# A norm's first load issued before the attention results' loads, and attention's value products with a mixed base and stacked half-width corrections

## The chip, the core and the metric

The kernel runs on one core of a Trainium2 chip. The metric is the device time of one execution in microseconds (us), as a median over runs. One profiled execution of the kernel before is the source of all durations; engines are called as in the profile: PE (matrix products; PEld is its weight load), DVE (vector), ACT (scalar), POOL, and SP, which here only issues transfers.

## The reference

The program computes one step of a decoder layer for a prompt of 1024 tokens and 8 samples of 8 tokens each (together T = 1088 columns), in 32-bit floats, model width 1024:

```
xn = RMSNorm(x)
[q | k | v | glu_a | glu_b | gate_a | gate_b] = xn @ w_in
A  = window attention (window 128, 16 heads on 4 key-value heads, a learned sink per head) @ w_o_attn
B  = silu(LayerNorm(causal depthwise conv of 31 taps (glu_a * sigmoid(glu_b)))) @ w_pb
h  = x + (sigmoid(gate_a) * A + sigmoid(gate_b) * B) @ w_out
y  = h + convolutional feed-forward of RMSNorm(h); then a final RMSNorm
```

For a prompt query i of a block of 128, the window holds the keys j <= i of its own block and the keys j > i of the block before. So over a "ring" of 128 key places each place holds either the own or the previous block's key, and the output is sum over j of p[i, j] * (v_own[j] if j <= i, else v_prev[j]).

## The kernel before

**Number form.** A 32-bit operand is split in a high part (a rounded copy, type fp32r) and a low part (operand minus high part). `split_ps` (L244) does this with a copy on ACT (L245) and a subtraction on DVE (L246). A full product is three matmuls (`mm3`, L208: high-high L210, high-low L211, low-high L212).

**Order of the work.** A weight of 128 output rows is one "stream" (L214): for each of three chunks of 384, 384 and 320 columns it runs eight steps of three matmuls, and evacuates the bank. Each step calls `tick` (L562), which first issues all steps of the agenda that are due. So attention, the layer norm and weight splits are woven into the streams at tick counts written out by hand: per attention unit values at 8 (`A_VALUES`), scores at 0 and 5, transposition ("turn") at 14 and 20, the value products ("mix") at 21 and 27; units follow each other at distances of 19 to 22 ticks. A framework then schedules the whole program at build time: it fixes each engine's order, by the order in which the program issues instructions, shifted by `later(offset)` (L140; a negative offset is sooner), and by its own estimate of when they are ready, and it puts in all waits. The convolution is issued with `CONV_LATER` = 1200, so it fills what DVE has left.

**Weights.** `w_load` (L154) issues the load of a weight on SP (L159, tile `wraw`, two buffers), two weights ahead. For weights after the first five of the input projection `w_parts` (L167) makes the low part without DVE: ACT casts (L181) and negates (L182), and a transfer on POOL's queue adds the weight from memory to it (L183).

**Attention** (`attn_unit`, L424) is done for two pairs of key-value heads (p = 0, 1), eight blocks each, and two groups g of four heads in each unit. `values` (L434) splits the block's v into `vt[:, 0]` and, if there is a block before, the difference d = v_prev - v_own into `vt[:, 1]`. `scores` (L442) are products of 256 columns (L451, L452) followed by a softmax over the ring (ACT L418, L422). `turn` (L459) transposes p on PE (L463), splits it into a high and a low part (tile `pt`), and, with a block before, multiplies both by the mask j > i (one DVE instruction over 1024 elements, L471). `mix` (L476) runs two or four matmuls of 128 x 512 (L482): v with both parts of p, and d with both masked parts. Their output rows hold the high and the low half of v; an ACT copy (L487) and a DVE addition (L488) sum them. After g = 1 the result is split into q's own place (L491, L492) and its low part is completed by a transfer on POOL (L493). Units of samples (`sample_unit`, L510) are woven in the same way; their transposed p is copied by ACT (L536) to a tile of tag "av", which the units' results use too.

**After attention** (L1010 to L1028): when two gate weights are left, the agenda is drained, attention's pools are closed, and the results of p = 0, which were spilled to memory, are read back by six transfers on SP, three of `ah` (L1022) and three of `al` (L1023). With the last gate weight the layer norm of the convolution's outputs begins. Its four parts (`ln_steps`, L610) each have a `load` (two transfers `ct` <- `d_c`, L636), `first` (sums on DVE, L622), `center` (a mean over the channels as a product on PE, L630, that waits for the sums; subtraction L646; squares on ACT, L649; sums) and `apply` (the second mean on PE, L630 again; root and reciprocal L384 and L385; scaling L662; silu L664; splits). `LN_AT` (L88) has the ticks of the four steps, counted from the start of the last gate weight. After it come the streams of the attention output projection (`do_o`, L1066), which first load the stored gate rows `ga` (L1068) and take their sigmoid on ACT (L1069); their first operand is `ah`.

## Time and profile before

| | |
|---|---|
| median of three runs | 1641.32 us (1641.26 to 1644.25) |
| the profiled execution: its time | 1641.11 us |
| its span in the trace | 1639.3 us |
| PE busy | 1621.9 us (99%) |
| DVE, ACT, POOL busy | 1342.9 (82%), 911.9 (56%), 314.3 us (19%) |
| mean clock granted to PE | 0.997 |
| the value products (L482) | 120, first at 221, last at 592 us |
| the norm's loads (L636) | 8, from 610 to 692 us |

How to read the rows in the prediction: a row of the order in time has the start and the length in us, the engine, the line of the code, the operation, output <- input by tile names, the shape and a count; in brackets stands how long the engine was idle before, and what ended that. A row of waits has who waited <- for whom: total us, times, longest. A row of one line's instructions has the shortest, median and longest duration in ns. PE's durations overlap, since matmuls are pipelined: their cost is the distance from start to start. "SPq" is SP's queue of transfers.

### The profile page before, as it was taken

To read this page: it belongs to the slowest core of one execution; us is meant where nothing else is said; L and a number is where in the kernel's file an instruction comes from. 1 tells how busy PE (TensorE), PEld (TensorE's weight loads), DVE (VectorE), ACT (ScalarE), POOL (GpSimd) and SP (SyncE) were. 2 spreads that over 40 slices of the span, in tenths; PEclk is the share of its full clock that TensorE was granted. 3 is DMA by queue.
4 is the path that set the end of the run, shared out by engine and by line. 5 is a ranking of instruction groups with operands and counts; after the bars stand their busy time and mean duration, and the time that the engine had idled before them with its cause. 6 is when DMAs were issued, how large, how long until landed. Compare 5 with 4: busy or idle time off the path is not lost.

```text
span 1639.3 us, 30059 instructions
## 1 busy us (share of the span) xinstructions
PE 1621.9 (99%) x11428; PEld 1603.7 (98%) x11428; DVE 1342.9 (82%) x2395; ACT 911.9 (56%) x1964; POOL 314.3 (19%) x579
## 2 busy tenths in 40 slices
PE   9999999999999999999999999999999999999998
PEld 9999999999999998999999999999999999999997
DVE  7879669999999825788755999988888877989767
ACT  6536387885678854676532465555555555524332
POOL 0211122322133321111102432222222111000000
PEclk9999999999999999999999999999999999999999
DMA  6455455748645576548763632344444334766313
GB/s 211 106 130 122 102 117 91 169 84 193 143 92 127 130 187 219 175 157 229 185 228 105 212 119 68 110 120 118 119 117 115 100 110 152 247 162 158 108 62 110
DMA packets 124249, 229.90 MB, mean 140 GB/s; under 512 B 28360, under 2 KB 70344, under 8 KB 124088
## 3 DMA queue, kind: packets, MB, share of 16 engines
q1 hardware_dynamic: 88536, 140.12, 27.9%
q0 software_dynamic: 35136, 87.45, 23.2%
q8 instruction: 90, 1.47, 0.4%
q14 instruction: 55, 0.45, 0.1%
q10 hardware_dynamic: 432, 0.40, 0.1%
HBM read 157.47 MB, written 64.03 MB: 135 GB/s over the span
## 4 chain that ended last, share of the span: by engine, by line
PE 81%; DVE 5%; issue 5%; ACT 4%; DMA 3%; POOL 1%; SPq 0%; POOLq 0%; DVEq 0%; ACTq 0%
PE mm L212 19%; PE mm L210 19%; PE mm L211 19%; PE aux L210 6%; PE aux L212 6%; PE aux L211 6%; PE aux L482 1%; ACT ct L664 1%; DMA ct<-d_c 1%; ACT p L418 1%; PE aux L463 1%; PE aux L451 1%; PE aux L452 1%; DVE c L584 0%; DMA q<-av 0%
## 5 line engine op out<-in xcount | busy, mean ns | idle before, releaser
L210 PE MATMUL mm<-xh,whi 128*128 128x384 f32 (+1 forms) x904 | 300.7, 333 | 0.2 <-ACT xh L299 0.2
L212 PE MATMUL mm<-xh,wlo 128*128 128x384 f32 (+1 forms) x904 | 296.8, 328 | 0.9 <-DMA wlo<-wall 0.9
L211 PE MATMUL mm<-xl,whi 128*128 128x384 f32 (+1 forms) x904 | 297.1, 329 | 0.4 <-DVE xl L300 0.4
L211 PEld LDWEIGHTS mm<-xl,whi 128*128 128x128 f32 x904 | 170.9, 189 | 2.6 <-DVE xl L300 0.9
L210 PEld LDWEIGHTS mm<-xh,whi 128*128 128x128 f32 x904 | 170.9, 189 | 2.1 <-ACT xh L299 0.7
L212 PEld LDWEIGHTS mm<-xh,wlo 128*128 128x128 f32 x904 | 170.7, 189 | 2.1 <-DMA wlo<-wall 1.2
L1474 DVE SCALAR_TENSOR_TENSOR acc<-st,fc,acc 128x1104 f32<-128x1104 f32 x88 | 119.9, 1366 | 12.2 <-issue 6.7
L212 PE MATMUL mm<-th,wlo 128*128 128x272 f32 x320 | 92.3, 289 | 0.0
L211 PE MATMUL mm<-tl,wlo 128*128 128x272 f32 x320 | 92.3, 288 | 0.0
L210 PE MATMUL mm<-th,wlo 128*128 128x272 f32 x320 | 92.2, 288 | 0.0
L584 DVE SCALAR_TENSOR_TENSOR bt<-u,consts,bt 128x513 f32<-128x513 f32 x120 | 90.0, 750 | 0.5
L584 DVE SCALAR_TENSOR_TENSOR c<-sm,hsum,c 128x512 f32<-128x512 f32 x120 | 89.6, 746 | 0.1
L212 PE MATMUL mm<-mh,wlo 128*128 128x272 f32 (+4 forms) x304 | 88.9, 292 | 0.0
L584 DVE SCALAR_TENSOR_TENSOR c<-u,consts,c 128x512 f32<-128x512 f32 x112 | 83.6, 746 | 0.4 <-ACT c L595 0.3
L245 ACT CAST whi<-wraw 128x512 fp32r<-128x512 f32 x76 | 47.5, 625 | 62.8 <-DVE wraw L1670 29.9
L1819 ACT COPY st<-mm 128x272 f32<-128x272 f32 (+2 forms) x132 | 43.8, 349 | 55.9 <-PE mm L212 55.9
L245 ACT CAST wlo<-wraw 128x512 fp32r<-128x512 f32 x76 | 47.3, 624 | 41.0 <-PE mm L212 17.4
L1472 ACT ACTIVATE acc<-st,fc 128x1104 f32<-128x1104 f32 x44 | 57.6, 1315 | 15.3 <-DVE st L1775 11.8
L210 PE MATMUL aux<-mh,whi 128*128 128x272 f32 (+4 forms) x216 | 63.8, 295 | 0.0
L211 PE MATMUL aux<-ml,whi 128*128 128x272 f32 (+4 forms) x216 | 63.5, 294 | 0.0
L181 ACT CAST whi<-wraw 128x1024 fp32r<-128x1024 f32 x37 | 38.8, 1049 | 41.7 <-PE mm L211 40.6
L246 DVE TENSOR_TENSOR wlo<-wraw,wlo 128x512 fp32r<-128x512 f32 x76 | 52.8, 695 | 9.8 <-ACT wlo L245 9.1
(723 smaller groups left out, 5806.9 us busy)
## 6 DMA issues: line engine op xcount, KB each, us to landing
wraw<-wall SPq DMA_DIRECT2D x118, 512.0 KB, 3.9
wlo<-wall POOLq DMA_DIRECT2D x37, 512.0 KB, 6.6
bw<-d_b SPq DMA_DIRECT2D x42, 272.0 KB, 3.7
d_b<-gd POOLq DMA_DIRECT2D x36, 272.0 KB, 6.1
d_b<-acc POOLq DMA_DIRECT2D x24, 272.0 KB, 4.8
ar<-wdn SPq DMA_DIRECT2D x32, 192.0 KB, 3.9
d_g<-acc POOLq DMA_DIRECT2D x10, 544.0 KB, 4.8
ct<-d_c SPq DMA_DIRECT2D x8, 544.0 KB, 7.6
```

What stands on the lines that cost most here:

```text
L181: self.cast = self.nc.scalar.copy(h, r).ins
L210: mm(ps, wh, xh, start=first, stop=False, skip_group_check=more)
L211: mm(ps, wh, xl, start=False, stop=False, skip_group_check=more)
L212: self.last_mm = mm(ps, wl, xh, start=False, stop=last, skip_group_check=more).ins
L245: self.cast = self.nc.scalar.copy(h, src).ins
L246: self.low = self.nc.vector.tensor_tensor(l, src, h.bitcast(F32), ALU.subtract).ins
L418: nc.scalar.activation(pt[:, j, 0:WIN + 1], pt[:, j, 0:WIN + 1], AF.Exp, bias=nm[:, j:j + 1], accum_out=den[:, j:j + 1])
L451: nc.tensor.matmul(ps[:, j, :], q[g][:, h, qs], kd[g][:, keys], start=True, stop=False)
L584: mac = lambda o, x, w: nc.vector.scalar_tensor_tensor(o, x, w, o, ALU.mult, ALU.add)
L1472: nc.scalar.activation(acc, st[:, 0:AW], AF.Identity, bias=fb(f), scale=fw(f, 0))
L1474: nc.vector.scalar_tensor_tensor(acc, st[:, k:k + AW], fw(f, k), acc, ALU.mult, ALU.add)
L1819: self.evicted = (add if second and n == 0 and j == 1 else op)(d, r(banks[bank, j]))
```

## The change

Four things are changed.

1. **Value products.** The base of the ring is now mixed: rows 0 to 63 of `vt` are the own block's, rows 64 to 127 those of the block before. For queries of the first half (x = 0) only keys 0 to 63 can be wrong then, for the second half only keys 64 to 127. So a correction needs 64 keys for 64 queries of each of four heads; the high and the low part of the masked p are stacked on the 128 rows (`ptc`), against a tile `two` that holds the difference's 64 rows twice. `two` is filled by four transfers on SP from a tile `s` (tag "ts"). The mask `below` gets signs: the correction of the second half is own minus previous. p is transposed with its columns ordered by half, head, query, and the evacuation turns them back. A mix has two products of 512 columns and two of 256.
2. **The norm's first load** is issued right after the drain, ahead of the loads of `ah` and `al`; its `first` is due at tick 0 instead of 1 and its `center` at 15 instead of 17.
3. **Weight splits** of the kind L180 to L183 are issued with an offset of -100 (`WEIGHTS_SOONER`).
4. **The samples' transposed p** gets a tile of tag "ts" in place of "av".

```diff
@@ -72,6 +72,7 @@
 A_TURN = (14, 20)
 A_MIX = (21, 27)
 SPILL = 10
+WEIGHTS_SOONER = -100
 THIRD = 6
 S_STEPS = (0, 12, 18)
 NORM_LATER = (0, 0, 0, 42)
@@ -85,7 +86,7 @@
 W_PARTS = 4
 CONV_LATER = 1200
 TURN_SOONER = -60
-LN_AT = ((0, 1, 17, 36), (2, 37, 50, 80), (60, 81, 103, 134), (90, 135, 152, 183))
+LN_AT = ((0, 0, 15, 36), (2, 37, 50, 80), (60, 81, 103, 134), (90, 135, 152, 183))
 LEAD = (0, 0)
 FIRST_UNIT = (10, 16)
 SPACING = ({"u": 22, "s": 13}, {"u": 19, "s": 13})
@@ -178,9 +179,10 @@
         self.w_hl.append((h, l))
         if FIRST < i < self.n_in:
             def whole():
-                self.cast = self.nc.scalar.copy(h, r).ins
-                self.nc.scalar.activation(l, h.bitcast(F32), AF.Identity, scale=-1.0)
-                self.nc.gpsimd.dma_start(l, self.a["wall"][i], accum_op=ALU.add)
+                with self.later(WEIGHTS_SOONER):
+                    self.cast = self.nc.scalar.copy(h, r).ins
+                    self.nc.scalar.activation(l, h.bitcast(F32), AF.Identity, scale=-1.0)
+                    self.nc.gpsimd.dma_start(l, self.a["wall"][i], accum_op=ALU.add)
             return [whole]
 
         def part(x):
@@ -432,12 +434,18 @@
         vals = {}
 
         def values():
-            vt = vals["vt"] = self.t(self.at, [P, 2, 4, HD], "vt", F32R, bufs=2)
-            self.split_ps(vt[:, 0, 0:4:3, :], vt[:, 0, 1:3, :], self.v[:, blk, p])
+            vt = vals["vt"] = self.t(self.at, [P, 4, HD], "vt", F32R, bufs=2)
+            for r, y in ((slice(0, HD), blk), (slice(HD, P), blk - 1)) if blk else ((slice(0, P), 0),):
+                self.split_ps(vt[r, 0:4:3, :], vt[r, 1:3, :], self.v[r, y, p])
             if blk:
                 d = self.t(self.at, [P, 2, HD], "vd")
                 nc.vector.tensor_tensor(d, self.v[:, blk - 1, p], self.v[:, blk, p], ALU.subtract)
-                self.split_ps(vt[:, 1, 0:4:3, :], vt[:, 1, 1:3, :], d)
+                s = self.t(self.at, [P, 4, HD], "ts", F32R)
+                self.split_ps(s[:, 0:4:3, :], s[:, 1:3, :], d)
+                two = vals["two"] = self.t(self.at, [P, 2, 4, HD], "two", F32R, bufs=2)
+                for x in range(2):
+                    for y in range(2):
+                        nc.sync.dma_start(two[y * HD:y * HD + HD, x].bitcast(F32), s[x * HD:x * HD + HD].bitcast(F32))
 
         def scores(g):
             pt = live[g]["pt"] = self.t(self.at, [P, 4, WIN + 4], "p", bufs=2)
@@ -461,31 +469,39 @@
             ps = self.bank("aux")
             for h in range(4):
                 nc.tensor.transpose(ps[:, h * P:(h + 1) * P], pt[:, h, 0:P], self.ident)
-            x = self.t(self.at, [P, 2, 512], "pt", F32R)
-            parts = [(0, x[:, y]) for y in range(2)]
+            x = self.t(self.at, [P, 2, 2, 4, HD], "pt", F32R)
+            ph, pl = live[g]["parts"] = x[:, 0], x[:, 1]
             with self.later(TURN_SOONER if self.now - self.gated <= 3 else 0):
-                self.split_ps(x[:, 0], x[:, 1], ps)
+                self.split_ps(ph, pl, ps.rearrange("p (h x q) -> p x h q", h=4, x=2))
                 if blk:
-                    below = self.masks[:, None, WIN:2 * WIN].to_broadcast([P, 8, WIN])
-                    x0 = self.t(self.at, [P, 2, 512], "pt0", F32R)
-                    nc.vector.tensor_tensor(x0.rearrange("p y (a b) -> p (y a) b", a=4),
-                                            x.bitcast(F32).rearrange("p y (a b) -> p (y a) b", a=4), below, ALU.mult)
-                    parts += [(1, x0[:, y]) for y in range(2)]
-            live[g]["parts"] = parts
+                    c = live[g]["c"] = self.t(self.at, [P, 2, 4, HD], "ptc", F32R)
+                    side = self.masks[:, WIN:2 * WIN].rearrange("p (x q) -> p x q", x=2)
+                    pick = lambda o, x, m: nc.vector.tensor_tensor(o, x.bitcast(F32), m, ALU.mult)
+                    pick(c, ph, side[:, :, None, :].to_broadcast([P, 2, 4, HD]))
+                    for x in range(2):
+                        r, o = [slice(y * HD, (y + 1) * HD) for y in (x, 1 - x)]
+                        pick(c[o, x], pl[r, x], side[r, x, None, :].to_broadcast([HD, 4, HD]))
 
         def mix(g):
             r, o = [slice(x * HD, (x + 1) * HD) for x in (g, 1 - g)]
             av = self.bank("aux")
-            parts = live[g]["parts"]
-            for n, (y, x) in enumerate(parts):
-                v = vals["vt"][:, y, 2 * g:2 * g + 2, :].rearrange("p x d -> p (x d)")
-                nc.tensor.matmul(av, v, x, start=n == 0, stop=n == len(parts) - 1)
+            ph, pl = live[g]["parts"]
+            pair = lambda v: v[:, 2 * g:2 * g + 2, :].rearrange("p x d -> p (x d)")
+            flat = lambda x: x.rearrange("p a h q -> p (a h q)")
+            nc.tensor.matmul(av, pair(vals["vt"]), flat(ph), start=True, stop=False)
+            nc.tensor.matmul(av, pair(vals["vt"]), flat(pl), start=False, stop=True)
+            if blk:
+                for x in range(2):
+                    nc.tensor.matmul(av[:, x * 256:x * 256 + 256], pair(vals["two"][:, x]),
+                                     live[g]["c"][:, x].rearrange("p h q -> p (h q)"), start=False, stop=True,
+                                     skip_group_check=True)
             if g == 0:
                 live[0]["t"] = self.t(self.at, [P, 4 * P], "av", bufs=2).rearrange("p (a b) -> p a b", a=4)
             t = live[0]["t"]
-            av = av.rearrange("p (a b) -> p a b", a=4)
-            nc.scalar.copy(t[r], av[o])
-            nc.vector.tensor_tensor(t[r], av[r], t[r], ALU.add)
+            rows = lambda x: x.rearrange("p h (x q) -> p x h q", x=2)
+            cols = lambda x: x.rearrange("p (x h q) -> p x h q", x=2, h=4)
+            nc.scalar.copy(rows(t[r]), cols(av[o]))
+            nc.vector.tensor_tensor(rows(t[r]), cols(av[r]), rows(t[r]), ALU.add)
             if g == 1:
                 h, l = q[0][:, :, qs], q[1][:, :, qs]
                 nc.scalar.copy(h, t)
@@ -532,7 +548,7 @@
             tr = self.bank("aux")
             nc.tensor.transpose(tr[:, 0:P], pt[:, 0, 0:P], self.ident)
             nc.tensor.transpose(tr[:, P:2 * P], pt[:, 0, 64:192], self.ident)
-            ts = live["ts"] = self.t(self.at, [P, 4 * P], "av", bufs=2)[:, 0:2 * P]
+            ts = live["ts"] = self.t(self.at, [P, 2 * P], "ts")
             nc.scalar.copy(ts, tr[:, 0:2 * P])
 
         def mix():
@@ -655,7 +671,7 @@
             self.rstd(rstd, ps)
             self.ln_apply(i, n, live["ct"], rstd)
 
-        return [(self.now + at, f) for at, f in zip(LN_AT[i], (load, first, center, apply))]
+        return [(at, f) for at, f in zip(LN_AT[i], (load, first, center, apply))]
 
     def ln_apply(self, i, n, ct, rstd):
         nc = self.nc
@@ -1016,16 +1032,15 @@
                 a0_es = ExitStack()
                 a0 = pool(a0_es, "a0")
                 self.lt = pool(a0_es, "lt")
+                norms = [self.ln_steps(x) for x in range(KT // 2)]
+                norms[0].pop(0)[1]()
                 ah = self.t(a0, [P, 4, T], "ah", F32R)
                 al = self.t(a0, [P, 4, T], "al", F32R)
                 for (o, w) in CHUNKS:
                     nc.sync.dma_start(ah[:, :, o:o + w].bitcast(F32), self.d_ah[:, :, o:o + w].rearrange("j p t -> p j t"))
                     nc.sync.dma_start(al[:, :, o:o + w].bitcast(F32), self.d_al[:, :, o:o + w].rearrange("j p t -> p j t"))
             if n == self.n_in - 1:
-                steps = []
-                for x in range(KT // 2):
-                    steps += self.ln_steps(x)
-                self.plan(steps)
+                self.plan([(self.now + at, f) for steps in norms for at, f in steps])
             if kind == "b":
                 u = do_b(i)
             elif kind == "a":
@@ -2134,13 +2149,14 @@
 
     r = np.arange(P)
     ii, jj = r[:, None], np.arange(2 * WIN)[None]
-    above, below = [x.astype(np.float32) for x in (jj[:, :WIN] > ii, jj[:, :WIN] < ii)]
+    above = (jj[:, :WIN] > ii).astype(np.float32)
+    below = np.where(jj[:, :WIN] < HD, (jj[:, :WIN] < ii) & (ii < HD), -1.0 * ((jj[:, :WIN] >= ii) & (ii >= HD)))
     b, t = r // HD, r % NT
     past = np.arange(WIN)[None] > t[:, None]
     n = np.arange(NS)[None]
     new = [(n // NT == (2 * bp + b)[:, None]) & (n % NT <= t[:, None]) for bp in range(4)]
     ok = np.concatenate([past] + new, 1)
-    return np.concatenate([above, below, np.where(ok, 0.0, -1e30).astype(np.float32)], 1)
+    return np.concatenate([above, below.astype(np.float32), np.where(ok, 0.0, -1e30).astype(np.float32)], 1)
 
 
 def pack_consts(i):
```

## The prediction

> **What bounds the kernel now.** I read the page first, then who PE waited for, then the stretches, then order in time around each place where PE stood.
>
> ```profile
> PE 1621.9 (99%) x11428; PEld 1603.7 (98%) x11428; DVE 1342.9 (82%) x2395; ACT 911.9 (56%) x1964; POOL 314.3 (19%) x579
> ```
>
> ```profile
> PE aux L630 <- DVE sm L622: 3.8, 1, 3.8
> PE aux L451 <- ACT av L536: 1.7, 1, 1.7
> PE mm L212 <- DMA wlo<-wall: 0.9, 1, 0.9
> ...
> PE aux L482 <- DVE pt L246: 0.2, 1, 0.2
> ```
>
> ```profile
> 260.00:540.00 280.00, 276.39 (x1730) 268.15 (x1730) 270.67 (x486) 209.46 (x548) 70.96 (x102) 1.00 0.59 130
> 540.00:600.00 60.00, 60.00 (x380) 58.33 (x379) 37.16 (x75) 46.59 (x135) 18.90 (x28) 1.00 0.57 125
> 600.00:620.00 20.00, 20.00 (x125) 20.00 (x124) 0.00 (x0) 5.15 (x8) 3.67 (x6) 1.00 1.02 337
> ```
>
> PE has work nearly everywhere, so PE time that is taken out counts, and so do its few waits; the second view (total, times, longest) holds those that this change can touch. In the stretches the columns are length, then busy time of PE, PEld, DVE, ACT and POOL, granted clock, DMA share and GB/s. During attention DVE is nearly as full as PE (270.67 of 280), but it has 22.8 us free in 540 to 600 and is wholly free in 600 to 620, where the DMA engines are full (1.02, 337 GB/s). So attention is bound by PE with DVE close behind, and the stretch around 620 by transfers.
>
> **Part 1: the corrections on PE.** Each of 28 mixes (14 units with blk > 0, two groups) had four products of 512 columns; now it has two of 512 and two of 256. The matmul's own duration misleads, since matmuls overlap; what counts is the distance from start to start.
>
> ```profile
> 235.72 1.10 PE L482 MATMUL aux<-pt,vt 128*128 128x512 f32 x4
> 236.65 0.34 PE L210 MATMUL mm<-xh,whi 128*128 128x384 f32 x1
> ```
>
> ```profile
> 502.77 0.28 PE L451 MATMUL aux<-kd,q 128*128 128x256 f32 x1
> 503.01 0.28 PE L451 MATMUL aux<-kd,q 128*128 128x256 f32 x1
> ```
>
> ```profile
> L482 PEld LDWEIGHTS aux<-pt,vt x120: 186/188/247, 220.9 to 591.5; 128*128 128x128 f32 x120
> ```
>
> Four products took 236.65 - 235.72 = 0.93, 0.232 us each. One 256-column score product (L452) lies between the two L451 rows, so 0.12 each. 56 products times (0.232 - 0.12) is **6.2 us** off PE. Bounds: 0.12 is for the same shape with a weight load of its own, so more than this is hardly to be had; the other end is that the weight load of 188 ns sets the spacing, 56 x (0.232 - 0.188) = 2.5 us. I take 6.2, since the nearest row (L451) is of the very shape.
> The Trainium skill, "TensorE: Matmul & The Clock Gate", section "Back-to-back issue gap", speaks against this size: it gives about 131 ns per product at 512 columns and 81 ns at 128 for a sustained stream of weight loads and products, so halving could save at most 50 ns, 2.8 us in all, and the forecast would be 1632.4. The trace disagrees: 232 ns at 512 columns.
>
> **Part 2: what the corrections cost elsewhere.**
>
> ```profile
> L246 DVE TENSOR_TENSOR pt<-aux,pt 128x512 fp32r<-128x512 f32 x32 | 22.0, 688 | 6.2 <-ACT pt L245 6.1
> L471 DVE TENSOR_TENSOR pt<-pt,masks 128x1024 fp32r<-128x1024 f32 x28 | 34.1, 1217 | 0.3
> ```
>
> ```profile
> 625.11 0.44 DVE L622 TENSOR_TENSOR u<-u 128x272 f32<-128x272 f32 x1
> ```
>
> ```profile
> L246 DVE TENSOR_TENSOR vt<-vd,vt x14: 262/284/291, 186.8 to 558.0; 128x128 fp32r<-128x128 f32 x14
> ```
>
> ```profile
> L828 SPq DMA_DIRECT2D q<-ql x24: 461/462/1632, 76.9 to 442.2; - x24
> DMA to landing us min/median/max: 2.0/3.6/7.7
> ```
>
> ```profile
> 231.74 0.29 DVE L246 TENSOR_TENSOR vt<-vd,vt 128x128 fp32r<-128x128 f32 x1
> ```
>
> In each turn one DVE product over 1024 elements (1.217) becomes one over 512 (0.69) and two over 256 (about 0.42 each, an estimate from 272 elements in 0.44): +0.31, 28 times 8.7 us. The values step splits in two halves, one DVE and one ACT instruction more in 14 units: 14 x 0.284 = 4.0 us on DVE, about as much on ACT. So DVE gets some 12.7 us. What it does at low urgency here is the convolution (issued 1200 places later), which can run on into the 42.8 us that DVE is free between 540 and 620; in 260 to 540 alone only 9.3 us are free. I cost it at nothing while that cover lasts.
> The new tile `two` needs four transfers on SP's queue in each of 14 units. By the L828 rows (also 64 partitions to the other half): four issues of 0.46 and 3.6 us to land, 5.4 us. In the first unit that has a correction the low part of the difference ended at 232.03 and the third product came at 235.72 + 2 x 0.232 = 236.2, a slack of 4.2; a wait of 1.2 us there. The DVE chain before a mix is 0.31 longer too. New waits lie between 0 and 5.6 us (28 mixes, 0.2 each), I take **+1.5**, near the lower end, because PE's order is fixed at build time, with these instructions in it, and in before PE waited for DVE ahead of a mix once, 0.2 us.
>
> **Part 3: two waits that go.**
>
> ```profile
> 476.66 1.31 POOL L493 DMA_DIRECT2D q<-av  x1 [0.62 <-ACT pt L245]
> ```
>
> ```profile
> 484.56 0.37 ACT L536 COPY av<-aux 128x256 f32<-128x256 f32 x1 [2.60 <-DMA q<-av]
> ```
>
> ```profile
> 373.29 0.90 POOL L183 DMA_DIRECT2D wlo<-wall  x1 [2.00 <-ACT q L245]
> ```
>
> At 484.56 the sample unit's copy waited for a buffer of tag "av" that the transfer issued at 476.66 was still reading, and PE waited for that copy: 1.7 us. The copy now has its own tag "ts", which the values step shares; so **-1.7**. What is late next there is the score copies behind it on ACT, of the same moment, so part may return (within the +1.5 above). The 0.9 us for wlo: its transfer went out on POOL at 373.29, behind work of other lines on ACT and POOL, and came 0.9 too late. WEIGHTS_SOONER puts cast, negation and transfer 100 places earlier: **-0.9**, since 0.9 is all that is missing. Pushed back are softmax work on ACT, which has 70 us free in 260 to 540, and on POOL, which may now stand waiting for a negation, the q<-av transfers and the rows of gates; what they write is read later, and the buffer that they hold is no longer L536's.
>
> **Part 4: the norm's first load.**
>
> ```profile
> 625.68 0.34 PE L212 MATMUL mm<-xh,wlo 128*128 128x384 f32 x1
> 629.82 1.24 PE L630 MATMUL aux<-sm,mean 128*128 128x272 f32 x2 [3.80 <-DVE sm L622]
> 630.47 0.85 PE L210 MATMUL mm<-xh,whi 128*128 128x320 f32 x1
> ...
> 635.57 0.30 PE L210 MATMUL mm<-xh,whi 128*128 128x320 f32 x1
> 636.00 0.31 PE L210 MATMUL mm<-xh,whi 128*128 128x320 f32 x1
> 642.21 0.62 PE L630 MATMUL aux<-sm,mean 128*128 128x272 f32 x2
> ```
>
> ```profile
> 593.96 0.33 SPq L159 DMA_DIRECT2D wraw<-wall  x1
> 598.15 0.38 SPq L1022 DMA_DIRECT2D ah<-d_ah  x1
> 609.85 14.24 SPq L636 DMA_DIRECT2D ct<-d_c  x4
> ```
>
> ```profile
> 630.34 0.73 DVE L622 TENSOR_TENSOR u<-ct 128x544 f32<-128x544 f32 x1 [0.32 <-DMA ct<-d_c]
> 631.58 2.42 DVE L646 TENSOR_TENSOR ct<-ct,aux 128x2176 f32<-128x2176 f32 x1
> 640.46 0.30 DVE L622 TENSOR_TENSOR sm<-c 128x136 f32<-128x136 f32 x1
> ```
>
> ```profile
> 631.62 1.28 ACT L1069 ACT_TABLE_LOAD   x1 [9.20 <-DMA ga<-d_ga]
> 635.30 1.10 ACT L649 ACTIVATE c<-ct 128x1088 f32<-128x1088 f32 x1
> ```
>
> The loads of ct stood behind six loads of attention results, and PE stood from about 626 to 629.82 for the first mean. After it, 18 products of 320 columns (630.47 up to 635.57) took 5.1 us where three took 0.43 at 635.57 (0.145 each). From 625.68 to 635.57 are 9.9 us; a last 384-column product (0.17), the mean pair (0.62, as at 642.21) and 18 x 0.145 are 3.4. So the wait and the slow spell behind it cost **6.5 us**. The Trainium skill, "TensorE: Matmul & The Clock Gate", section "Part 1: The HAM clock gate", says that an idle window of about 3.4 us halves the clock; the trace agrees (0.28 per product, then 0.145).
> In the changed kernel the two transfers (8 x 128 x 136 x 4 bytes each by the code, 1.1 MB together) leave ahead of `ah`. By the sizes of the tiles, ct's first buffer lies over `ql` and `p`, and the last unit's transposes are the last to read those, so SP can issue it before 598.15, about where it issued the weights at 593.96. What it is moved past on SP, six loads of ah and al and the weights behind them, lands at most 3.3 us later (1.1 MB at 337 GB/s); the first product on ah comes after 636.00, 38 us after its issue. First sums then come early and the first mean doesn't wait, also not two ticks (1.04 us) sooner. But the chain behind it still passes the full queue: DVE took the second piece's sums (630.34) before the centering (631.58), ACT waited for `ga` until 631.62 before the squares (635.30), and the second mean was ready at 640.76, against 642.21 when PE came. With 1.1 MB fewer in the queue all these come 3.3 us earlier: 637.5. PE comes 6.5 us earlier: 635.7. So PE waits 1.7 there, too short for another slow spell (260 to 540 holds waits of 1.7 and 0.9 and has a clock of 1.00): **+1.7**, between 0 and 5.1 (no shift of the queue).
>
> **The sum**, against the profiled execution's own 1641.11 (0.2 from the median of the runs shown): 1641.1 - 6.2 - 1.7 - 0.9 + 1.5 - 6.5 + 1.7 = **1629.0**.
>
> **Rivals.**
> 1. *The wait moves from the first mean to the second.* If ct's load leaves no sooner than 598.15, the queue is as full as before, the centering stays at 631.58 and the second mean at 640.76, and PE at 635.7 waits 5.1 us and falls into a slow spell (18 products at 0.28 instead of 0.145, 2.5 us): part 4 gives -6.5 + 5.1 + 2.5 = +1.1 in place of -4.8. Time 1634.9. For it: SP's order is strict, and DVE's and ACT's orders are laid down at build time. Against: nothing that ct needs is late. Chance 0.20.
> 2. *DVE becomes the bound in attention.* If the convolution cannot slide past 540 (its buffers are wanted by later b streams), the stretch needs 12.7 us more of DVE with 9.3 free: +3.4 instead of parts 1 to 3, with part 4 at -4.8: 1639.7. Against: the last b stream evacuates into its buffer at 454.64, and after that none is wanted.
>
> ```profile
> 454.64 0.48 ACT L766 COPY u<-mm 128x256 f32<-128x256 f32 x2
> ```
>
> Chance 0.09.
> 3. *Slower: `two` stands behind weights in SP's queue.*
>
> ```profile
> SPq L159 <- ACT whi L181: 250.4, 26, 23.9
> ```
>
> SP stood 9.6 us on average at a weight load until ACT had cast the weight before. A transfer of `two` queued behind such a load comes 9.6 + 5.4 = 15.0 after its operand, with 4.2 of slack: PE waits 10.8 us. One such unit leaves 1639.8, about no change; from two on it is slower: 1629.0 + 2 x 10.8 = 1650.6. Against: the q transfers go through the same queue and no wait of PE is put down to them. Chance 0.10.
> 4. *The weight load sets the spacing of narrow products* (part 1's other bound, the mechanism that the page's rule implies): 1629.0 + 3.7 = 1632.7. Chance 0.03: L451 speaks against it.
>
> **How the numbers follow.** The forecast has 0.58. A change of 0.2% (3.3 us) is about what a measurement of this kernel can tell. Faster: forecast 0.58, rival 1 with 0.19, rival 2 with 0.02, rival 4 with 0.03, together 0.82. Same: rest of rival 1 (0.01) and of rival 2 (0.07), 0.08. Slower: rival 3, 0.10. The range: with no new waits at all 1629.0 - 1.5 - 1.7 = 1625.8, rounded down to 1625 for the weight load's own spacing (0.12 may be a little less). Above: rival 1 with attention's waits at their bound, 1634.9 + 4.1 = 1639; left out are rival 3 and most of rival 2.
>
> **What would show it.** Right: L482's successors at 0.12 from start to start for 256 columns; no row for L536 nor for wlo among PE's waits; ct's first issue before ah's; the clock at 1.00 throughout 620 to 640; a wait of one or two us at the second mean. Wrong: a wait over 3.4 us at the second mean with a clock below 1 after it (rival 1); `two` among PE's releasers (rival 3); convolution past 600 with ct waiting for d_c (rival 2); PE waits on `ptc` products adding up to more than 5 us.

## The result, and the profile after

The changed kernel took 1646.39 us (median of 20 runs, 1643.20 to 1650.28) beside 1641.39 for the kernel before on the same chip (20 runs): a ratio of 1.0031, 95% interval [1.0023, 1.0038]. It is slower by 0.3%, some 5 us; forecast were 1629.0, at most 1639.0. The profiled execution took 1646.8 us, its span is 1645.0 (before 1639.3). The busy times of its page:

```profile
PE 1622.3 (99%) x11428; PEld 1600.9 (97%) x11428; DVE 1356.8 (82%) x2465; ACT 916.4 (56%) x1978; POOL 315.4 (19%) x579
```

DVE has 13.9 us more (estimated: 12.7). PE is as long busy as before; that says little, since a product's own duration grows where it is slow (0.52 us in place of 0.34 at half clock, rows of e10 in the last section). Who PE waited for (total, times, longest):

```profile
PE mm L214 <- DMA wlo<-wall: 6.7, 2, 3.6
PE aux L495 <- DMA two<-ts: 4.0, 2, 2.6
PE aux L471 <- ACT p L424: 2.1, 2, 1.8
...
PE aux L495 <- DVE ptc L479: 0.8, 2, 0.5
PE aux L646 <- DVE sm L638: 0.6, 2, 0.4
```

The 3.8 us at the first mean and the 1.7 us at the samples' copy are gone. In their place stand waits for `two`, the new tile, and for `wlo`, the low part of weights, which was to come sooner. The three stretches of the prediction (PE, PEld, DVE, ACT, POOL, clock, DMA share, GB/s):

```profile
260.00:540.00 280.00, 270.54 (x1691) 261.61 (x1691) 265.86 (x509) 208.26 (x546) 69.86 (x101) 0.99 0.61 136
540.00:600.00 60.00, 58.66 (x371) 54.91 (x370) 53.08 (x113) 46.89 (x140) 16.75 (x26) 1.00 0.57 133
600.00:620.00 20.00, 20.00 (x122) 19.59 (x121) 5.12 (x12) 5.96 (x12) 3.46 (x5) 1.00 0.83 228
```

DVE did not fit its new work into 260 to 540 (it did 265.86 us there, 4.8 less than before, since the others held it up); the work slid, as supposed, into 540 to 600 (53.08 in place of 37.16) and past 600. But PE lost time on the way. Where, is seen from how much later (+) or sooner (-) the same stream product starts than in the kernel before. The columns are instants of the kernel before; attention ends at about 604, the first mean lies between 604 and 641, the second shortly behind 641. The other rows are experiments, told below. Each row rests on one profiled execution, and executions of one kernel lie several us apart (before: 1637.80 to 1645.16), so a difference of one or two us in it carries no weight alone.

| run | 297 | 409 | 604 | 641 | 704 | 781 |
|---|---|---|---|---|---|---|
| the whole change | +4.1 | +7.3 | +8.8 | +7.7 | +8.5 | +7.4 |
| e1, attention alone | +6.2 | +10.2 | +9.6 | +10.0 | +11.1 | +10.5 |
| e4, half the transfers | 0.0 | +1.8 | +0.9 | -1.1 | +1.1 | +1.2 |
| e12, no low picks | +5.0 | +3.7 | +0.2 | -2.5 | -1.9 | -1.1 |
| e8, both | -0.4 | -1.1 | -5.8 | -11.1 | -6.4 | -7.4 |
| e2, norm alone | +0.3 | +0.5 | +0.3 | -2.0 | 0.0 | -0.8 |
| e7, norm behind a chunk | -0.2 | -0.3 | -0.8 | -7.4 | -0.1 | +2.4 |
| e5, all but corrections | -0.1 | +4.3 | +1.7 | -2.8 | +2.3 | +0.8 |
| e13, norm and tag | +0.7 | +0.2 | -1.9 | -6.0 | -3.3 | -2.5 |

In the whole change attention loses 8.8 us where 7.3 were to be won; the norm wins about 1. (Behind the last stream product the program takes 7.4 us in the profiled execution of before, 6.1 here and 6.1 to 6.3 in 13 of the 15 experiments: these 1.3 us belong to that execution, not to the change.) The first loss, 3.4 us between 256 and 297, lies here; the rows are from the order in time, of SP, ACT, DVE and PE:

```profile
253.05 0.33 SPq L160 DMA_DIRECT2D wraw<-wall  x1
256.45 2.73 SPq L448 DMA_DIRECT2D two<-ts  x4
```

```profile
264.33 0.30 ACT L247 CAST ts<-vd 128x128 fp32r<-128x128 f32 x1 [3.97 <-DMA two<-ts]
```

```profile
264.66 0.29 DVE L248 TENSOR_TENSOR ts<-vd,ts 128x128 fp32r<-128x128 f32 x1 [3.04 <-ACT ts L247]
```

```profile
263.98 0.36 PE L495 MATMUL aux<-ptc,two 128*128 128x256 f32 x1 [2.59 <-DMA two<-ts]
...
266.46 0.47 PE L213 MATMUL mm<-xl,whi 128*128 128x320 f32 x1
266.73 0.47 PE L214 MATMUL mm<-xh,wlo 128*128 128x320 f32 x1
...
269.15 0.31 PE L212 MATMUL mm<-xh,whi 128*128 128x320 f32 x1
269.30 0.31 PE L213 MATMUL mm<-xl,whi 128*128 128x320 f32 x1
```

The four transfers leave at 256.45, 3.4 us behind a 512 KB weight load on the same queue. They land 5.7 to 6.9 us after their issue (3.4 is the median of all of them), and their readers go on only at 264, 7.5 us after the first issue. Their source, the tile of tag "ts", has one buffer. So it is not PE alone that waits: ACT stands 3.97 us at the next unit's cast into that buffer, with other work of attention behind it, and DVE stands 3.04 for ACT. Behind PE's 2.59 us the products of 320 columns start 0.27 us apart, later 0.15: a spell at half clock. The second loss, 3.2 us between 297 and 409, is a wait of 3.06 us for `wlo` at 400 (its row is in the last section).

### The profile page after: what moved, and what is told of

The parts are those of the page before. It is cut to its first block, busy times and chain, and to the rows that moved or that the text cites. A ratio compares the mean times of both kernels' runs of the same rounds, so it can differ in the third digit from the quotient of the medians.

```text
span 1645.0 us, 30301 instructions
## 1 busy us (share of the span) xinstructions
PE 1622.3 (99%) x11428; PEld 1600.9 (97%) x11428; DVE 1356.8 (82%) x2465; ACT 916.4 (56%) x1978; POOL 315.4 (19%) x579
## 4 chain that ended last, share of the span: by engine, by line
PE 81%; DVE 6%; DMA 5%; ACT 3%; issue 3%; POOL 1%; SPq 0%; POOLq 0%; DVEq 0%; ACTq 0%
PE mm L214 19%; PE mm L212 19%; PE mm L213 19%; PE aux L214 7%; PE aux L213 7%; PE aux L212 7%; DMA wlo<-wall 2%; DVE c L600 1%; DMA two<-ts 1%; DVE bt L600 1%; DMA d_c<-u 1%; DVE ptc L479 1%; ACT p L420 1%; DMA ct<-d_c 1%; PE aux L459 1%
## 5 line engine op out<-in xcount | busy, mean ns | idle before, releaser
L1489 DVE SCALAR_TENSOR_TENSOR acc<-st,fc,acc 128x1104 f32<-128x1104 f32 x88 | 119.8, 1365 | 12.2 <-issue 6.7
L1487 ACT ACTIVATE acc<-st,fc 128x1104 f32<-128x1104 f32 x44 | 57.6, 1315 | 14.5 <-DVE st L1790 11.8
L185 POOL DMA_DIRECT2D wlo<-wall x37 | 33.6, 909 | 160.5 <-ACT wlo L184 113.2
L183 ACT CAST whi<-wraw 128x1024 fp32r<-128x1024 f32 x37 | 38.9, 1051 | 40.2 <-PE mm L213 39.0
```

The lines of the kernel that those rows point to most:

```text
L183: self.cast = self.nc.scalar.copy(h, r).ins
L185: self.nc.gpsimd.dma_start(l, self.a["wall"][i], accum_op=ALU.add)
L1487: nc.scalar.activation(acc, st[:, 0:AW], AF.Identity, bias=fb(f), scale=fw(f, 0))
L1489: nc.vector.scalar_tensor_tensor(acc, st[:, k:k + AW], fw(f, k), acc, ALU.mult, ALU.add)
```

## What the experiments should tell apart

Theory T: the loss comes from the transfers of `two` and the single buffer behind them, and the norm's gain is eaten by the weights' transfers that it collides with. Rivals: U, the sooner weights turn the order of ACT's and POOL's queues against PE; V, DVE's new work binds attention (the prediction's rival 2); X, the corrections do save what was forecast, and only the stand at `ts` ate it. Ratios are to the kernel before on the same chip, with 95% intervals; the last column is the ratio less one, times 1640 us. "Half" means half the transfers (e4), "no low" that the low part's picks and so that part of the corrections are left out.

| run | median us | ratio | us |
|---|---|---|---|
| the whole change | 1646.39 | 1.0031 [1.0023, 1.0038] | +5.1 |
| e1 attention parts and tag | 1649.85 | 1.0057 [1.0042, 1.0071] | +9.3 |
| e2 norm | 1637.80 | 0.9981 [0.9973, 0.9990] | -3.1 |
| e3 weights | 1640.05 | 0.9996 [0.9987, 1.0006] | -0.7 |
| e4 whole, half | 1641.19 | 1.0006 [0.9996, 1.0016] | +1.0 |
| e5 norm, weights, tag | 1640.11 | 1.0004 [0.9996, 1.0013] | +0.7 |
| e6 attention parts and tag, half | 1645.80 | 1.0035 [1.0023, 1.0047] | +5.7 |
| e7 norm, load behind a chunk | 1641.54 | 1.0011 [1.0002, 1.0019] | +1.8 |
| e8 whole, half, no low | 1632.04 | 0.9953 [0.9940, 0.9966] | -7.7 |
| e9 whole, half, low picks on POOL | 1664.24 | 1.0145 [1.0130, 1.0159] | +23.8 |
| e10 e8 with idle picks | 1640.71 | 1.0002 [0.9992, 1.0012] | +0.3 |
| e11 before with idle picks | 1644.50 | 1.0024 [1.0015, 1.0034] | +3.9 |
| e12 whole, no low | 1639.90 | 0.9996 [0.9985, 1.0006] | -0.7 |
| e13 norm, tag | 1635.69 | 0.9972 [0.9961, 0.9982] | -4.6 |
| e14 e4 without sooner weights | 1642.19 | 1.0016 [1.0007, 1.0025] | +2.6 |
| e15 e8 without sooner weights | 1630.79 | 0.9944 [0.9932, 0.9957] | -9.2 |

## Experiments 1 to 4: the parts, and the transfers

**e1, e2 and e3** take the edits apart: attention (with the tag), the norm's load, the sooner weights (`WEIGHTS_SOONER = -100`), each on the kernel before.

> The attention products, the picks, the transfers of two and the samples' tag alone; weights and norm as before. Theory T (the loss comes from the transfers of two, whose source ts has one buffer, so that ACT stands at the next unit's cast and PE at the corrections): slower than before by 2 to 5 us (narrow products -3, waits for two +4, a spell of half clock behind them +1.7, the first mean's wait of 3.8 stays), with waits of PE for two of 2 to 5 us in all and none of over 1.5 us for wlo. Rival U (the sooner weights make the loss by turning the order of ACT's and POOL's queue): faster by 3 to 5 us, since the sooner weights are away. Rival V (DVE's 13 us more bind attention): slower by 4 to 8, with PE's waits naming the picks and the adds of DVE, more than 3 us in all.

> The norm's first load alone. T: the wait of 3.8 us at the first mean goes, but the gate rows' writes then share the DMA engines with the load and wlo of the last gate stream comes late: net 0 to -2.5 us, a wait for wlo of 1 to 3.6 us near 630. U: wlo is late only because of the sooner weights, so here the load costs nothing: -3.5 to -6 us, no wait for wlo near 630.

> The sooner weights alone. T: within 1.5 us of before; no wait for wlo of over 1 us beyond those of before. U: +3 to +6 us, with waits for wlo of about 3 us near 400 and near 630.

e1 lost more than T or V had expected, +9.3. The same place as above, of ACT, DVE and PE:

```profile
264.17 0.30 ACT L247 CAST ts<-vd 128x128 fp32r<-128x128 f32 x1 [5.24 <-DMA two<-ts]
```

```profile
264.50 0.29 DVE L248 TENSOR_TENSOR ts<-vd,ts 128x128 fp32r<-128x128 f32 x1 [5.05 <-ACT ts L247]
264.82 0.87 DVE L479 TENSOR_TENSOR ptc<-pt,masks 64x256 fp32r<-64x256 f32 x2
```

```profile
265.30 1.03 PE L495 MATMUL aux<-ptc,two 128*128 128x256 f32 x2 [4.83 <-DVE ptc L479]
```

Read alone, PE's row blames DVE's pick `ptc`. But the pick had been standing behind the low part of `ts`, this behind ACT, and ACT behind the transfers: one stand goes through three engines in order. U fell as an explanation of the whole loss: without the sooner weights attention lost more, and these alone (e3) changed nothing that can be measured. e2 gained 3.1, between T's 0 to 2.5 and U's 3.5 to 6: the first mean no longer waits, but PE waits for `wlo` at 609 instead, and 1.42 us for a later mean, at 693, so that the 2.0 us that it is ahead at 641 are gone at 704:

```profile
609.01 0.69 PE L212 MATMUL mm<-xh,wlo 128*128 128x384 f32 x1 [2.61 <-DMA wlo<-wall]
```

That weight's transfer left at 596.80, as before (596.56), but now `ct` is on its way too, which left at 594.72: the weight's transfer took 12.2 us to land, 8.6 before.

**e4** keeps the whole change, but splits the half of the difference that stays on its partitions straight into `two`; only the crossing halves are transferred, and the tile `s` is gone.

```diff
-                s = self.t(self.at, [P, 4, HD], "ts", F32R)
-                self.split_ps(s[:, 0:4:3, :], s[:, 1:3, :], d)
                 two = vals["two"] = self.t(self.at, [P, 2, 4, HD], "two", F32R, bufs=2)
                 for x in range(2):
-                    for y in range(2):
-                        nc.sync.dma_start(two[y * HD:y * HD + HD, x].bitcast(F32), s[x * HD:x * HD + HD].bitcast(F32))
+                    r, o = [slice(y * HD, (y + 1) * HD) for y in (x, 1 - x)]
+                    self.split_ps(two[r, x, 0:4:3, :], two[r, x, 1:3, :], d[r])
+                    nc.sync.dma_start(two[o, x].bitcast(F32), two[r, x].bitcast(F32))
```

> The whole change, but the half of each unit's difference that stays on its partitions is split straight into two, and only the two crossing halves are transferred (two of the four transfers, no tile ts for the values). T: ACT no longer stands at the cast for the transfers (before this 10.0 us in 4 waits), PE's waits for two fall from 4.0 us to under 1 us and the spell of half clock near 264 goes: 3 to 5 us less than the whole change, 1641 to 1643.5. U and V: no gain of over 1 us (1645.5 to 1646.5), since weights and picks are as in the whole change.

It came out as T expected: 4.1 us less than the whole change, no wait of PE for `two`, and nothing lost at 297. So the stand at `ts` costs about 4 us; e4 takes away half the transfers and the single source buffer at once, and does not tell their shares apart. But that leaves the change 1 us above before, not 12 below.

## Experiments 5 to 12: what the corrections cost without the stand

**e5** is everything but the corrections; **e6** is e1 with half the transfers; **e7** puts the norm's load between the first and the second chunk of `ah` and `al`; **e8** is e4 without the loop over the two picks of the low part, so that the corrections leave that part out:

```diff
-                    for x in range(2):
-                        r, o = [slice(y * HD, (y + 1) * HD) for y in (x, 1 - x)]
-                        pick(c[o, x], pl[r, x], side[r, x, None, :].to_broadcast([HD, 4, HD]))
```

> All of the change except the corrections: the norm's load, the sooner weights and the samples' tag on the products of before. The loads alone gave -2.0 us and the weights alone +0.2, the tag takes away a wait of 1.7 us near 485. Theory T (the corrections are what costs; beside the stand at ts they save only 2.4 us of PE and give that back in late operands): 1636 to 1638. Rival X (the corrections save the 6.2 us forecast, and only the stand at ts ate it): then the whole change with half the transfers, 1641.2, would have to be 6 us below this kernel, so this one would have to stand at 1645 or above.

> The attention products, picks and samples' tag alone with two of the four transfers (the half that stays is split straight into two), weights and norm as before. If the parts add up, it is the run of the whole change with half the transfers less the norm's -2.0: 1642 to 1643.5 (T). X: 1634 to 1636.

> The norm's first load alone, put between the first chunk of ah and al and the second, not ahead of all three. T (ahead of all three it takes bandwidth from the wlo and the gate rows that the next gate stream waits for, a wait of 2.6 us at 609): that wait falls under 0.5 us, the first mean still has no wait, 2 to 3 us less than with the load ahead of all: 1635 to 1636.5. Rival (wlo and the gate rows are late through ah and al themselves): as the load ahead of all, 1637 to 1638.5.

> The whole change with half the transfers, and without the two picks of the low part (that part of the corrections is left out of the sum). DVE does 28 x 0.86 = 24 us less in attention. T with DVE's order as the cause (PE waits for ptc at the weight load, so narrow products take 0.22 in place of 0.12): PE's waits for ptc fall, 2 to 4 us less: 1637.5 to 1639. If DVE's work is hidden and only PE's own products count: within 1 us of 1641.2.

X fell: e5 stands at 1640.1, so even without the stand the corrections win nothing (e4 1641.2, against e5). With the weights as before they even cost 7.2 us (e14, +2.6, against e13, -4.6). T's number for e5 was missed too (below), and e6 came out 2.3 us above its range, since the parts do not add up. The large step is e8: 8.7 us less than e4, more than the 2 to 4 expected. The two picks are 24 us of DVE's time in attention, but no more than 2.9 us of PE's narrow products: from start to start, waits left out, the 56 of them take 9.7 us in the whole change, 10.2 in e4 and 7.3 in e8. The rows show the difference, first of e8, then of DVE, PEld and PE in e4:

```profile
242.09 0.40 PE L491 MATMUL aux<-ptc,two 128*128 128x256 f32 x2
242.33 0.34 PE L213 MATMUL mm<-xl,whi 128*128 128x384 f32 x1
```

```profile
514.03 0.87 DVE L478 TENSOR_TENSOR ptc<-pt,masks 64x256 fp32r<-64x256 f32 x2
```

```profile
514.50 0.19 PEld L494 LDWEIGHTS aux<-ptc,two 128*128 128x128 f32 x1 [0.34 <-DVE ptc L478]
```

```profile
514.50 0.39 PE L494 MATMUL aux<-ptc,two 128*128 128x256 f32 x1
514.73 0.34 PE L212 MATMUL mm<-xh,whi 128*128 128x384 f32 x1
514.96 0.39 PE L494 MATMUL aux<-ptc,two 128*128 128x256 f32 x1
515.18 0.34 PE L213 MATMUL mm<-xl,whi 128*128 128x384 f32 x1
```

A pair whose operands lie ready takes 0.24, 0.12 each, as forecast. In e4 here the weight load, 0.19, starts only when the pick is done, together with its product, so it is not hidden, and each product takes 0.22 to 0.23. (Behind a transpose a narrow product takes 0.20 even where `ptc` has long been ready, in e8 too.) So is it the late operand or DVE's time? **e10** makes the two picks again, but into a tile that no one reads (64x224, for lack of space; the corrections leave the low part out as in e8). **e11** adds such picks to the kernel before. **e9** moves the real ones to POOL (`nc.gpsimd` in place of `nc.vector`), with nothing left out.

> The whole change with half the transfers, and the two 64x256 picks of the low part on POOL in place of DVE (nothing left out). Theory V (DVE's 24 us of low picks delay ptc and all that stands behind them on DVE): near the kernel without them, 1632 to 1636, if POOL takes under 1 us for one and is not standing at a DMA when it is due; narrow products near 0.13 us each. If leaving the low part out helped by chance of order alone: 1638 to 1645. If POOL's own queue holds the picks up: PE waits for ptc from POOL of more than 4 us and over 1641.

> The whole change with half the transfers, the two picks of the low part made by DVE at the same place in its order, 64x224, but into a tile that nobody reads; the corrections leave the low part out. DVE has 22 of the 24 us again, PE waits for none of it. If DVE's time is what costs (its queue), 1639 to 1641; if only the wait of the narrow products for their operand costs, as the kernel without these picks: 1632 to 1634.

> The kernel before with the same two 64x256 picks a group more on DVE, into a tile that nobody reads: 28 x 0.85 = 24 us more of DVE in attention. V, DVE near its bound there (352 of 407 us busy before): slower by 4 to 10 us. If DVE has room: within 1.5 us of before.

The stretch of attention, 200 to 600, of before, e4, e8, e10 and e11 in turn; the third number behind the comma is DVE:

```profile
200.00:600.00 400.00, 396.39 (x2498) 385.50 (x2497) 351.76 (x643) 303.98 (x812) 108.39 (x159) 1.00 0.58 125
```

```profile
200.00:600.00 400.00, 393.88 (x2494) 380.88 (x2494) 369.57 (x725) 311.38 (x836) 105.85 (x159) 1.00 0.57 130
```

```profile
200.00:600.00 400.00, 395.91 (x2536) 386.95 (x2535) 347.48 (x672) 312.17 (x836) 105.35 (x159) 1.00 0.60 133
```

```profile
200.00:600.00 400.00, 392.56 (x2488) 380.21 (x2487) 367.62 (x723) 311.29 (x835) 105.32 (x158) 1.00 0.57 129
```

```profile
200.00:600.00 400.00, 396.07 (x2476) 382.28 (x2475) 374.02 (x698) 301.15 (x807) 107.41 (x156) 1.00 0.55 123
```

e10 gives back 8.0 of e8's 8.7 us, although PE reads none of those picks and its narrow products take 7.2 us there as in e8: what costs is that the picks stand on DVE, not the wait for their result. e11 shows it on the kernel before: 24 us more of idle work, +3.9 us, just under V's 4 to 10. So V's forecast holds: DVE has gaps (88% busy in the kernel before, 351.76 of 400), yet each us of more work costs 0.16 us there and about a third beside the corrections.

By which path it costs is not shown. No single wait row shows it. PE loses it in pieces, in e10 (in brackets e8) 1.34 (0.92) us at a transpose at 343, 2.24 (1.17) for `wlo` at 394, 1.02 (none) at a score at 564 and 2.65 (1.09) for `wlo` at 622, with half clock behind both waits for `wlo`; of these only the score's row names DVE, and e8 gives 2.29 back at the second mean. The largest single piece of e11 is a wait for `wlo`, too, 2.31 in place of 0.91, with 3.2 us of half clock behind it:

```profile
383.68 0.44 PE L212 MATMUL mm<-xh,wlo 128*128 128x384 f32 x1 [2.31 <-DMA wlo<-wall]
```

And a rival stays that no run excludes. The framework lays down the orders anew for each kernel: in e10, 28 of the 56 narrow products stand at another place between the stream products than in e8, and ACT's and POOL's orders differ as well. A change of order alone can be worth as much (5.3 us, e13 below). Against mere chance speaks that all five comparisons go one way: without the picks e8, e12 and e15 gain 8.7, 5.8 and 11.8 us, with idle ones e10 and e11 lose 8.0 and 3.9.

POOL was no way out: its queue holds the picks up, the last of e9's three expectations. PE waits for it 30 times; the rows are POOL's group, then PE's wait:

```profile
L478 POOL TENSOR_TENSOR ptc<-pt,masks 64x256 fp32r<-64x256 f32 x56 | 49.6, 886 | 39.4 <-DVE ptc L478 31.7 <-DVE den L422 4.8 <-DVE den L410 0.4
```

```profile
PE aux L494 <- POOL ptc L478: 17.6, 30, 2.1
```

One pick takes 886 ns there, against a mean of 421 on DVE. The Trainium skill, "GPSIMD Engine Reference", section "4.1 Engine selection", gives about twice DVE's time for elementwise work with two inputs; the trace agrees (2.1).

**e12** closes the square with e4 and e8: four transfers, no low picks.

> The whole change, all four transfers from ts, without the two picks of the low part (that part of the corrections is left out). It closes a square: whole change 1646.4, half the transfers 1641.2, half the transfers without the low picks 1632.0. If the stand at ts and DVE's load are two costs that add (T and V): 1636 to 1639, with waits for two or ts still there. If the stand at ts only bites because DVE is full: 1632 to 1634. If the transfers cost the same 5 us but the picks nothing here: 1644 and above.

From the whole change (+5.1), half the transfers take 4.1 us, leaving out the picks 5.8 (e12 stands 0.9 us above the range of two costs that add), and both 12.8. They are two costs, and each is worth some 3 us more once the other is gone. PE's wait for `two` is still there in e12 (3.64 us at 264), so it needs no full DVE. Like e8, e12 is no rival to the kernel before, as it does less.

**e7** missed by 5 us, and shows the prediction's rival 1. One part came as T had it: the wait for `wlo` at 609 is gone, its transfer took 8.8 us (12.2 in e2), so it was the load ahead of everything that made it late. The norm's load came early enough, the first mean began at 623.97, 5.9 sooner than before, and PE ran 7.4 us ahead (table). Then, of DVE and PE:

```profile
629.07 0.73 DVE L622 TENSOR_TENSOR u<-ct 128x544 f32<-128x544 f32 x1 [0.45 <-DMA ct<-d_c]
630.30 2.42 DVE L646 TENSOR_TENSOR ct<-ct,aux 128x2176 f32<-128x2176 f32 x1
```

```profile
639.67 0.79 PE L630 MATMUL aux<-sm,mean 128*128 128x272 f32 x1 [4.75 <-DVE sm L622]
```

The centering stands on DVE behind the sums of the second piece, and these behind that piece's load. It comes at 630.30, 1.3 us sooner than before, so the second mean takes the wait over, with a spell of half clock of 3.5 us behind it.

## Experiments 13 to 15: why the parts do not add up

> The norm's load and the samples' tag, weights as before. The load alone gave 1637.8, load with tag and sooner weights 1640.1. If the sooner weights take the norm's gain back: 1636 to 1638. If the tag does: 1639.5 to 1641.

> The whole change with half the transfers, weights as before. With sooner weights 1641.2. If the sooner weights cost about 2 here too: 1638 to 1640. If they help once attention is late: 1642 to 1644.

> The whole change with half the transfers and without the two low picks (that part of the corrections is left out), weights as before. With sooner weights 1632.0; if these cost 2: 1629 to 1631; if they help: 1633 to 1635.

e13 is e5 without the sooner weights, and 5.3 us faster, 0.3 us beyond the range in which these take the norm's gain back. The tag does what was forecast: the wait at 485 is gone, and with the norm's load the kernel is 4.6 us below before. It is the fastest version here that computes all that the reference asks for. The sooner weights took that back. Alone (e3) they remove the same wait at 485 and put another at 397, so they seem harmless; with the tag only the new wait is left. Of e13, then of e5:

```profile
381.03 0.44 PE L212 MATMUL mm<-xh,wlo 128*128 128x384 f32 x1 [0.40 <-DMA wlo<-wall]
```

```profile
395.44 0.45 PE L214 MATMUL mm<-xh,wlo 128*128 128x384 f32 x1 [2.25 <-DMA wlo<-wall]
```

e5 has a spell of half clock behind that wait, and 4.3 us lost at 409 (table). The transfer that PE waits for there went out no sooner than in e13 (383.92 against 383.35), but took 11.5 us to land in place of 8.9. Beside the corrections the sign varies: with half the transfers the sooner weights win 1.6 us (e4 against e14), without low picks they lose 1.5 (e8 against e15), both near what can be told; e14 came out as "they help" had it, e15 as "these cost 2". Which order of the queues makes them so is not settled.

## Why the prediction was wrong, point by point

- **The corrections on PE** (-6.2). The price of 0.12 was right for operands that lie ready; with the picks late it is 0.17 to 0.18. Before, the 120 value products took 29.2 us from start to start; after, 64 wide ones 16.5 and 56 narrow ones 9.7. So 3.0 us were saved, and 5.2 (16.7 and 7.3) in e8.
- **What they cost elsewhere** (+1.5): the step that failed, twice. First, "I cost it at nothing while that cover lasts". The cover did last, the convolution slid into 540 to 600, and work on DVE still cost PE time, as e8, e10 and e11 show: at 88% to 92% busy it was not free, whether or not there was room later. By the prices of e11 and e10 the forecast's 12.7 us come to 2 to 5 us (an estimate; no run has just these). Rival 2 named the engine, but let it decide only where the stretch overflows. Second, the transfers: 5.4 us were reckoned, 7.5 passed, and the reckoning followed one reader, PE. The writer of the single source buffer, ACT at the next unit, was left out, although the text had seen just such a stand in the tag "av" (part 3) and moved the samples' copy into the same tag; without the stand the whole change is 4.1 us faster (e4). Together with the sooner weights these made +8.8 us at 604, where -7.3 was forecast.
- **Rival 3** came near with 1650.6, by another mechanism: in the unit that PE waited longest for, at 256, SP did not stand at a weight load, the transfers were issued at once, and landed late. (In the unit at 397 three of the four left 5.6 us behind the first, with a weight load between; PE did not wait for that one.) That the weight's bytes ahead on the same queue made them late is read from the order (1.6 us ahead in e1, 3.4 in the whole change), and was not tested.
- **The tag** (-1.7): right. e13 less e2 is -1.5.
- **The sooner weights** (-0.9): wrong. Alone they came to -0.7, with an interval of -2.1 to +1.0. The wait of 0.9 was seen to be short by 0.9, but what the offset pushes elsewhere was priced at nothing; a wait of 2.25 us came, beside norm and tag +5.3 us.
- **The norm's load** (-4.8 net): -3.1 alone. `ct` did leave ahead of `ah` (603.82 against 606.92), and the first mean had no wait. What failed is "lands at most 3.3 us later" for what is moved back: only SP's queue was followed, but the transfers on POOL's queue, the gate rows and `wlo`, came late, as e2 and e7 show for `wlo`. The +1.7 at the second mean did not come in e2, where PE was only 2.0 us sooner, not 6.5. In the whole change, of POOL, ACT and PE:

```profile
606.56 1.46 POOL L822 DMA_DIRECT2D d_ga<-gt  x1
```

```profile
619.15 0.48 ACT L244 COPY gt<-mm 128x384 f32<-128x384 f32 x1 [11.53 <-DMA d_ga<-gt]
```

```profile
630.47 0.56 PE L214 MATMUL mm<-xh,wlo 128*128 128x384 f32 x1 [3.60 <-DMA wlo<-wall]
```

  ACT stood 11.53 us for a buffer of gate rows that was still being written out (12.5 us, 5.9 in before for the gate rows that left at 610.81), cast the weight after that, and PE waited 3.60 us for its low part: the wait of the first mean under another name.
- **Rival 1** (the second mean takes over) holds where PE does come early: e7, and in the table each row that is far ahead at 641 has lost part of it by 704 (e8 4.7 us, e13 2.7, e5 5.1).

## What to carry to other kernels

Do not price work on an engine that is near full at nothing because it has room later; an idle instruction of the same size is a cheap test, though it also changes the orders that a framework lays down. For each new transfer, ask who will write its source next and how many buffers it has: an engine that works in order and stands there stops its other work (ACT for 5.24 us in e1, and DVE and PE behind it). Where a stretch is full of transfers, moving one load ahead can move the wait to whoever has a transfer under way then, on another queue too.

## What the runs showed of the hardware that was not expected

The forecast took 1.7 us of waiting as too short for a spell at half clock. Shorter waits than the 3.8 of the kernel before can bring one, but not always do. Rows of e10, then of the whole change:

```profile
622.54 0.45 PE L214 MATMUL mm<-xh,wlo 128*128 128x384 f32 x1 [2.65 <-DMA wlo<-wall]
...
623.71 0.34 PE L214 MATMUL mm<-xh,wlo 128*128 128x384 f32 x1
623.88 0.49 PE L212 MATMUL mm<-xh,whi 128*128 128x384 f32 x1
624.17 0.52 PE L213 MATMUL mm<-xl,whi 128*128 128x384 f32 x1
...
627.35 0.33 PE L214 MATMUL mm<-xh,wlo 128*128 128x384 f32 x1
```

```profile
400.06 0.44 PE L214 MATMUL mm<-xh,wlo 128*128 128x384 f32 x1 [3.06 <-DMA wlo<-wall]
400.35 0.34 PE L212 MATMUL mm<-xh,whi 128*128 128x384 f32 x1
400.52 0.34 PE L213 MATMUL mm<-xl,whi 128*128 128x384 f32 x1
```

In e10 the products were 0.17 us apart after the wait, then for 3.5 us (623.88 to 627.35) 0.32 apart; in the whole change they stayed at 0.17 after a longer wait. The shortest single wait with such a spell behind it was 1.96 us (e5, at 641.53), the longest without one this 3.06; in e9 two waits of 0.57 and 0.74 us close together (280.75 and 281.88) were enough. So a wait of two us can cost 3.5 in all. The Trainium skill, "TensorE: Matmul & The Clock Gate", section "Part 1: The HAM clock gate", puts the limit at an idle window of about 3.4 us and calls the window free-running; the length of the spells agrees, the limit on the wait does not.
